# Six transformer layers on one core: a first gathering of expert inputs in fp32, and low parts of weights moved at two joints of four layers

## Chip, core and metric

The kernel runs on one core of a Trainium2 chip. The metric is device time in microseconds (us) of one execution. TensorE multiplies matrices (PE in the profile, its weight loads PEld), VectorE is DVE, ScalarE is ACT, GpSimd is POOL, and SyncE (SP) asks for most transfers.

## What is computed

256 tokens of width 1024 pass through four layers and then two routed ones, all in fp32. Cut to what matters:

```
def first_block(...):
    for i in range(4):
        h = rmsnorm(x, g[0])
        y = diff_attention / nsa_attention / forgetting_attention (h, ...)   # by layer
        x = x + rmsnorm(y, g[1])
        y = sqrelu_mlp(rmsnorm(x, g[2]), mlp_w1[i], mlp_w2[i])        # width 4096
        x = x + rmsnorm(y, g[3])
        x = x + sigmoid(x @ ple_gate_w[i]) * (p[i] @ ple_w[i])

def second_block(...):
    for layer in range(2):
        hcur = rms_norm(x, norm1_g[layer]) * (1 + sc1) + sh1
        x = x + g1 * mixer(hcur)
        hcur = rms_norm(x, norm2_g[layer]) * (1 + sc2) + sh2
        x = x + g2 * hierarchical_moe(hcur, ...)
    return rms_norm(x, final_norm_g)

def hierarchical_moe(...):        # 16 experts; top group of 4, then top 2 in it
    for e in range(16):
        hid = silu(xt @ w_gate[e]) * (xt @ w_up[e])
        y = y + gates[:, e:e + 1] * (hid @ w_down[e])
```

## The kernel before

**Products in parts.** A matrix in fp32 is split into a high part (a rounded copy in the type fp32r, made by ScalarE) and a low part (what is missing, made by VectorE). A product is three products in fp32r: high by high, low by high, high by low. For weights, `whi` is the high part (L270, L277; 128x2048 in one instruction) and `wlo` the low one (L289; two instructions of 128x1024 for one piece, four for a unit of 1024 rows and 512 columns). For activations, `xTh` and `xTl` are evacuated from the PSUM buffer of the transposes (L434): ScalarE copies the high part, VectorE subtracts (both L423).

**Order.** The program is written as Python functions; a scheduler of the framework sets the order of each engine's queue from its own timeline, and `with self.behind(x)` asks it to place what follows after x. Each engine then runs its queue strictly in order.

**The first four layers** (`first_layer`). At the end of the mixer the two halves of 128 tokens are normalised (`enter`: L2202 scales, L2203 adds, into `tm`), transposed and fed to the MLP, whose first products are `mm_a` (L342). `update` (L2208, L2209) adds the mixer's result to the stream x behind that. This is the first joint. The MLP's second matrix is the products `pB<-whi,t` and `pB<-wlo,t` of L308; their sum is normalised in `post_norm` (sum of squares `ss` L396, the reciprocal root L360 to L384, L457 scales, L458 adds to x). x is transposed (L434), and the gate's products (L308 with `whi` or `wlo` and `xTh` or `xTl`) follow. Its first unit of weights is `ug`. This is the second joint.

**The routed layers** (`second_layer`, `moe_pass`). Each half's router logits (L2027) give, on VectorE, the chain of L1593 to L1615 (`route`), then the counts on TensorE (L1627), then 0/1 matrices `Dm` (L1642) that say which token sits in which place. A gathering (`gather`, `collect`, L1675) multiplies columns of X, as stationary operand, with `Dm`: the result, with a shift added by ScalarE (L1682), is `xg`, the transposed inputs of four experts in 256 columns. X is the normalised input in two parts (L2038 high, ScalarE; L2039 low, VectorE), both reordered while being written, so that column block k of X holds the features 8p + k. So a gathering has 8 k x 2 halves x 2 parts = 32 products.

There are 16 experts, two at a time (j = 0 to 7), and a gathering for every two j, four in a layer: the first ahead of j = 0, the second inside j = 1 between the products of gate and up (L1829) and the turn (L1746) to the product down, the third behind j = 3, the fourth inside j = 5. The experts' weights are used in plain fp32 (L1829), with four tiles of 32 columns of the array side by side. They come in pieces of 1 MB (four for gate, up and down each), asked for by SyncE as their buffers come free. A second part of the gathering for experts with more tokens than places (the block under `If` in `rest`) doesn't run in the profiled execution beyond its branch.

Of the kernel before, what the change touches and what calls it, by code (L numbers as in the profile page):

```python
# [21 lines left out]
D = 1024  # L22
# [30 lines left out]
class Net:  # L53
# [396 lines left out]
    def post_norm(self, y, g, h, r2):  # L450
# [4 lines left out]
        r = self.rstd(y, scale=r4, factor=r2)  # L455
        for n, yn in zip(HALVES, y):
            v.scalar_tensor_tensor(yn, yn, r, g[:, n], op0=OP.mult, op1=OP.mult)  # L457
            last = v.tensor_add(self.x[h][:, n], self.x[h][:, n], yn)  # L458
# [1209 lines left out]

    def collect(self, p, X, Dm, b, halves):

        for i in range(2):
            ks = slice((2 * b + i) * 128, (2 * b + i + 1) * 128)
# [114 lines left out]
    def expert_weights(self, l, name, j):  # L1787


        e = [self.expert(j, s) for s in range(2)]  # L1790
        src = self.a[f"moe_w_{name}_2"][l, e[0]:e[1] + 1:e[1] - e[0]]
        pieces = []
        for i in range(4):
            if name != "down":
                tag, n, k0 = "raw" if name == "gate" else "whi", slice(0, 512), 2 * i
                s = src.rearrange("s (p i k) n -> i p s k n", i=4, k=2)[i]
            elif j < 7:
                tag, n, k0 = "wlo", slice(0, D), i
                s = src[:, 128 * i:128 * i + 128].rearrange("s (k p) n -> p s k n", k=1)
            else:  # L1800
                tag, n, k0 = "wlo", HALVES[i // 2], 2 * (i % 2)
                s = src[:, 128 * k0:128 * k0 + 256, n].rearrange("s (k p) n -> p s k n", k=2)
            if name == "gate" and j % 2 and i < 2:
                t = self.xp.tile([128, 2, 2, 512], F32, name="xTl", tag="xTl", bufs=2)
            else:
                t = self.wt(tag, [128, 2, 1 if tag == "wlo" and j < 7 else 2, n.stop - n.start], F32)
            if name == "down" and j == 7:
                for e in range(2):
                    self.nc.sync.dma_start(t[:, e], s[:, e])
            else:  # L1810
                self.nc.sync.dma_start(t, s)
            pieces.append((t, k0, n))
        return pieces
# [19 lines left out]
    def moe_pass(self, l, X, R, sh, g2, first, weights, rest, late, ahead):  # L1833
# [14 lines left out]
        for j in range(8):  # L1848
# [17 lines left out]
            if c and j != 3 and q < 3:  # L1866
# [7 lines left out]
            if j == 6:  # L1874
                late()
            DT, (gs,) = place[j]
# [3 lines left out]
            if j == 3:  # L1880

                self.combine(acc, range(2), j, *out.pop(j))
                rest(acc)
# [6 lines left out]
    def moe_rest(self, l, X, R, sh, g2, base, acc):  # L1890
# [15 lines left out]
        for j in range(8):  # L1906
# [6 lines left out]
            for b in range(4):  # L1913
                p = self.pB([128, 2, 128])
                for i in range(2):
                    ks = slice((2 * b + i) * 128, (2 * b + i + 1) * 128)
                    for k in range(4):
                        h, part = divmod(k, 2)
                        nc.tensor.matmul(p[:, i], X[h][part][:, ks], Dm[:, h], start=k == 0, stop=k == 3)
# [19 lines left out]
    def moe(self, l, X, R, sh, g2, first, weights):  # L1939
# [3 lines left out]
        row = self.one([128, D], "next")  # L1943

        def late():
            self.bcast(self.a["final_norm_g_2"] if l else self.mod[1, D:2 * D], D, row)
# [12 lines left out]
        def rest(acc):  # L1959
# [27 lines left out]
        return update, row  # L1987

    def second_layer(self, l, mix, oT, after):
# [4 lines left out]
        y, begin, end = self.mixed(mix, oT, w, (l, 1 - l))  # L1994
        weights = {"gate": self.expert_weights(l, "gate", 0)}
# [386 lines left out]
```

## Time and profile before

| what | value |
|---|---|
| median of three runs | 2271.1 us (2264.89 to 2271.54) |
| the profiled execution | 2268.48 us, of it 2266.7 us span |
| TensorE (PE) busy | 2104.9 us, 93% |
| VectorE busy | 1346.7 us, 59% |
| ScalarE busy | 937.4 us, 41% |
| moved | 541.67 MB, mean 239 GB/s |

The profile is one execution. "Busy" counts what an engine computed; bracketed times in its rows are idle time just before an instruction, with what ended it. PEclk is the clock granted to TensorE as a share of full speed: 1.00 and 0.50 are its two levels, 2.4 and 1.2 GHz.

### The profile page before, as it was taken

How to read it: one execution, taken by the hardware profiler on the slowest of the kernel's cores; microseconds unless marked ns; L12 is line 12 of the kernel's file. 1: busy time of each engine (PE TensorE's matmuls, PEld its weight loads, DVE VectorE, ACT ScalarE, POOL GpSimd, SP SyncE). 2: the span in 40 equal slices, each digit the busy share in tenths (PEclk: the TensorE clock that was granted, in tenths of full speed). 3: DMA queues.
4: the chain of work that ended last, by engine and by line, in shares of the span. 5: the costliest groups of instructions: out<-in, count | busy, mean ns of one | idle time of the engine just before them, and what ended most of it. 6: DMA issues, size and time to landing. Idle time of an engine off the chain costs nothing. (4 is left out here: it accounts for less than half of the span.)

```text
span 2266.7 us, 35540 instructions
## 1 busy us (share of the span) xinstructions
PE 2104.9 (93%) x14072; PEld 1608.8 (71%) x14072; DVE 1346.7 (59%) x2794; ACT 937.4 (41%) x1464; POOL 25.2 (1%) x69
## 2 busy tenths in 40 slices
PE   7989999989999999999999899989898988989897
PEld 5868888976788878788888698978743327864332
DVE  4578767575877665877666787677611027851112
ACT  4545435455543455544445444446411115521111
POOL 0000000000000010000000000000000001000000
PEclk9999999999999999999999999999999998999999
DMA  8527774630587464477564387656599984469995
GB/s 296 182 74 253 268 257 171 212 121 29 191 279 278 169 217 155 173 260 267 202 229 161 87 284 261 215 205 205 225 407 418 420 353 155 152 246 420 418 419 225
DMA packets 246362, 541.67 MB, mean 239 GB/s; under 512 B 27501, under 2 KB 77189, under 8 KB 246181
## 3 DMA queue, kind: packets, MB, share of 16 engines
q1 hardware_dynamic: 242597, 533.98, 65.3%
q10 hardware_dynamic: 3552, 5.24, 0.6%
q8 instruction: 116, 1.90, 0.3%
q14 instruction: 65, 0.53, 0.1%
q0 software_dynamic: 32, 0.02, 0.0%
HBM read 533.36 MB, written 5.83 MB: 238 GB/s over the span
## 5 line engine op out<-in xcount | busy, mean ns | idle before, releaser
L289 DVE TENSOR_TENSOR wlo<-raw,whi 128x1024 fp32r<-128x1024 f32 x476 | 558.5, 1221 | 223.9 <-ACT whi L270 201.8
L270 ACT CAST whi<-raw 128x2048 fp32r<-128x2048 f32 x218 | 411.1, 1907 | 417.9 <-PE pB L308 336.8
L308 PE MATMUL pB<-whi,t 128*128 128x512 f32 x1088 | 308.1, 401 | 4.7 <-ACT t L423 3.2
L308 PE MATMUL pB<-xTl,whi 128*128 128x256 f32 x1600 | 257.0, 285 | 0.0
L308 PE MATMUL pB<-xTh,whi 128*128 128x256 f32 x1600 | 254.9, 288 | 0.4 <-ACT whi L270 0.4
L308 PE MATMUL pB<-xTh,wlo 128*128 128x256 f32 x1600 | 250.2, 284 | 0.0
L308 PEld LDWEIGHTS pB<-whi,t 128*128 128x128 f32 x1088 | 202.0, 191 | 49.0 <-ACT t L423 4.1
L308 PEld LDWEIGHTS pB<-xTh,whi 128*128 128x128 f32 x1600 | 218.8, 193 | 11.8 <-issue 8.6
L308 PEld LDWEIGHTS pB<-xTl,whi 128*128 128x128 f32 x1600 | 223.2, 193 | 5.3 <-issue 2.3
L308 PEld LDWEIGHTS pB<-xTh,wlo 128*128 128x128 f32 x1600 | 217.8, 192 | 2.7 <-issue 1.7
L308 PE MATMUL pB<-wlo,t 128*128 128x512 f32 x544 | 170.9, 395 | 0.0
L308 PE MATMUL pB<-whi,xTh 128*128 128x512 f32 (+1 forms) x512 | 145.0, 409 | 11.4 <-ACT xTh L423 9.3
L308 PE MATMUL pB<-whi,xTl 128*128 128x512 f32 (+1 forms) x512 | 143.5, 402 | 10.1 <-DVE xTl L423 6.7
L308 PE MATMUL pB<-wlo,xTh 128*128 128x512 f32 (+1 forms) x512 | 139.9, 395 | 0.0
L1195 DVE SCALAR_TENSOR_TENSOR adac<-adaw,cs,adac 128x512 f32<-128x512 f32 x168 | 125.8, 749 | 21.5 <-DMA adaw<-in_w_ada_dram 19.0
L1829 PE MATMUL pB<-wlo,t 128*32 128x512 f32 (+1 forms) x1024 | 116.6, 594 | 11.7 <-ACT t L1747 11.7
L1753 DVE SCALAR_TENSOR_TENSOR t<-pB,gs,g 128x512 f32<-128x512 f32 x32 | 24.0, 751 | 166.2 <-PE pB L1829 164.6
L308 PEld LDWEIGHTS pB<-whi,xTh 128*128 128x128 f32 x512 | 95.4, 197 | 37.2 <-ACT xTh L423 15.2
L308 PEld LDWEIGHTS pB<-whi,xTl 128*128 128x128 f32 x512 | 96.9, 198 | 34.6 <-DVE xTl L423 8.7
L308 PEld LDWEIGHTS pB<-wlo,t 128*128 128x128 f32 x544 | 103.0, 189 | 24.1
L1829 PE MATMUL pB<-whi,xg 128*32 128x512 f32 (+1 forms) x1024 | 114.4, 593 | 0.0
L308 PEld LDWEIGHTS pB<-wlo,xTh 128*128 128x128 f32 x512 | 96.0, 194 | 21.6 <-issue 2.7
(384 smaller groups left out, 2375.9 us busy)
## 6 DMA issues: line engine op xcount, KB each, us to landing
raw<-in_mlp_w_dram SPq DMA_DIRECT2D x128, 1024.0 KB
whi<-in_moe_w_up_dram SPq DMA_DIRECT2D x64, 1024.0 KB
wlo<-in_moe_w_down_dram SPq DMA_DIRECT2D x56, 1024.0 KB
adaw<-in_w_ada_dram SPq DMA_DIRECT2D x96, 512.0 KB
raw<-in_moe_w_gate_dram SPq DMA_DIRECT2D x48, 1024.0 KB
raw<-in_da_w_in_dram SPq DMA_DIRECT2D x24, 1024.0 KB
raw<-in_ple_gate_w_dram SPq DMA_DIRECT2D x16, 1024.0 KB
xTl<-in_moe_w_gate_dram SPq DMA_DIRECT2D x16, 1024.0 KB
```

What stands on the lines that cost most here:

```text
L270: done = nc.scalar.copy(hi, raw)
L289: last = subtract(lo[:, ks], raw[:, ks], hi[:, ks].bitcast(F32), OP.subtract)
L308: self.last_mm = self.nc.tensor.matmul(ps, l, r, start=start and i == 0, stop=stop and i == n - 1)
L1195: v.scalar_tensor_tensor(acc, t[:, i], self.cs[:, k + i:k + i + 1], acc, op0=OP.mult, op1=OP.add)
L1753: self.nc.vector.scalar_tensor_tensor(t, p, gs, g2[:, n], op0=OP.mult, op1=OP.mult)
L1829: self.last_mm = self.nc.tensor.matmul(out[u][es], xT[:, k0 + k, es], t[:, s, k, c], start=done[u] == 1, stop=done[u] == total[u], tile_po ...
```

## The change

Three things are changed.

**At the first joint**, the four L289 of the MLP's first unit `u1` leave the chain of `enter`: they stood ahead of a sum of squares and between the two adds L2203; now they are asked for behind the last transposes of the second half. Scaling and adding alternate (L2232, L2233 in the new numbering).

**At the second joint**, the four L289 of the gate's first unit `ug` are asked for behind the last add of `post_norm` to the first half; they stood ahead of `post_norm`. Here too scaling and adding alternate.

**In the routed layers**, X stays one fp32 matrix for each half, in the stream's own order of features, made by ScalarE alone (contiguous). The first gathering multiplies it in fp32: 16 products in the place of 32. The two parts are made later, at j = 1 (`in_parts`), and serve the other gatherings. Since X is no longer reordered, each gathering reads its stationary operand at a step of 8 elements (`some_rows`), the later ones too. The gathering of j = 1 goes behind the product down. Two of the gate's pieces for j = 1 are asked for early, one into the buffer that `in_parts` uses later; the row that was broadcast into a tile of its own ("next") goes into a recycled buffer of X.

```
-    def unit_apart(self, w, c0):
+    def unit_apart(self, w, c0, first=(), then=()):
         raws = [self.load(w[k * 512:(k + 1) * 512, c0:c0 + 512]) for k in range(2)]
-        u = [self.high(raw, 4 * k) for k, raw in enumerate(raws)]
-        for p, raw in zip(u, raws):
-            self.low(p, raw)
+        with self.behind(*first):
+            u = [self.high(raw, 4 * k) for k, raw in enumerate(raws)]
+        with self.behind(*then):
+            for p, raw in zip(u, raws):
+                self.low(p, raw)
...
+    def some_rows(x, k):
+        return x.rearrange("t (p k) -> t k p", k=8)[:, k]
+
+    def in_parts(self, X):
+        hi = self.one([128, 2, D], "hi", F32R)
+        parts = []
+        for h in range(2):
+            self.nc.scalar.copy(hi[:, h], X[h])
+            lo = self.one([128, D], "X", F32R, bufs=3)
+            self.nc.vector.tensor_tensor(lo, X[h], hi[:, h].bitcast(F32), OP.subtract)
+            parts.append([hi[:, h], lo])
+        return parts
...
-                for part in range(2):
-                    self.nc.tensor.matmul(p[:, i], X[h][part][:, ks], Dm[:, h].rearrange("p c s -> p (c s)"),
-                                          start=h == i == part == 0, stop=h == part == 1, skip_group_check=True)
+                places = Dm[:, h].rearrange("p c s -> p (c s)")
+                if len(X[h]) == 1:
+                    places = places.bitcast(F32)
+                for n, x in enumerate(X[h], 1):
+                    self.nc.tensor.matmul(p[:, i], self.some_rows(x, 2 * b + i), places, start=h == i == 0 and n == 1,
+                                          stop=h == 1 and n == len(X[h]), skip_group_check=True)
...
-            if c and j != 3 and q < 3:
+            if j == 1:
+                X = self.in_parts(X)
+            elif c and j != 3 and q < 3:
                 Dm, xg = self.whole(self.gather(R, X, sh, q + 1))
...
+            if j == 1:
+                Dm, xg = self.whole(self.gather(R, X, sh, q + 1))
+                put(q + 1)
...
         weights = {"gate": self.expert_weights(l, "gate", 0)}
+        self.asked["gate", 1, 0] = self.expert_piece(l, "gate", 1, 0)
...
+            self.asked["gate", 1, 2] = self.expert_piece(l, "gate", 1, 2)
...
-            X = [[self.one([128, D], f"X{h}{part}", F32R) for part in range(2)] for h in range(2)]
+            X = [self.one([128, D], "X", bufs=3) for h in range(2)]
...
-                x = xG[h].rearrange("t (p k) -> t k p", k=8)
-                hi, lo = (t.rearrange("t (k p) -> t k p", k=8) for t in X[h])
-                nc.scalar.mul(hi, x, r[h])
-                v.scalar_tensor_tensor(lo, x, r[h], hi.bitcast(F32), op0=OP.mult, op1=OP.subtract)
...
+            with self.behind(copied):
+                nc.scalar.mul(X[0], xG[0], r[0])
...
-            with self.behind(self.weighted):
-                for u, raw in zip(u1, raws):
-                    self.low(u, raw)
...
             last = self.transpose_in(xg[1], mT, 1)
             with self.behind(*last):
+                for u, raw in zip(u1, raws):
+                    self.low(u, raw)
                 update(y, 0, r0)
...
-            self.post_norm(Y[0], g3, 0, r2[0])
-            with self.behind(*last):
-                ug = [self.unit_apart(self.a["ple_gate_w"][i], 0)]
+            normed = self.post_norm(Y[0], g3, 0, r2[0])
+            ug = [self.unit_apart(self.a["ple_gate_w"][i], 0, last, normed)]
```

VectorE at the second joint of layer 0, before; `x_80` is x of the first half. The four L289 of `ug` stand as one row ahead of all of these:

```order
L457 SCALAR_TENSOR_TENSOR pB<-pB,ry_3380,tm 128x512 x2
L458 TENSOR_TENSOR x_80<-x_80,pB 128x512
L396 TENSOR_TENSOR ss<-ss 128x1
L458 TENSOR_TENSOR x_80<-x_80,pB 128x512
L360 TENSOR_SCALAR rx_3448<-ss,r_3439 128x1
L362 TENSOR_SCALAR rt_3449<-rx_3448 128x1
L364 TENSOR_SCALAR ry_3450<-rt_3449 128x1
L369 SCALAR_TENSOR_TENSOR rh_3451<-ry_3450,rx_3448 128x1
L423 TENSOR_TENSOR xTl<-pB,xTh 128x4x128
```

The same place after the change:

```order
L461 SCALAR_TENSOR_TENSOR pB<-pB,ry_3380,tm 128x512
L462 TENSOR_TENSOR x_80<-x_80,pB 128x512
L461 SCALAR_TENSOR_TENSOR pB<-pB,ry_3380,tm 128x512
L462 TENSOR_TENSOR x_80<-x_80,pB 128x512
L289 TENSOR_TENSOR wlo<-raw,whi 128x1024 x4
L398 TENSOR_TENSOR ss<-ss 128x1
L425 TENSOR_TENSOR xTl<-pB,xTh 128x4x128 x2
L289 TENSOR_TENSOR wlo<-raw,whi 128x1024 x2
```

The four L289 now stand between the second add to x and the two `xTl`, ahead of the second half's sum of squares `ss`.

VectorE at the first joint of layer 0, before (`t_1484` and `t_1487` are the scaled halves of the first 128 tokens' row):

```order
L2202 SCALAR_TENSOR_TENSOR t_1484<-pB,ry_1472,tm 128x512
L2202 SCALAR_TENSOR_TENSOR t_1487<-pB,ry_1472,tm 128x512
L2203 TENSOR_TENSOR tm<-tm,t_1484 128x512
L289 TENSOR_TENSOR wlo<-raw,whi 128x1024 x2
L2203 TENSOR_TENSOR tm<-tm,t_1487 128x512
```

After, first the same place and, behind the line of dots, what follows the last `xTl` of this joint:

```order
L2232 SCALAR_TENSOR_TENSOR t_1484<-pB,ry_1472,tm 128x512
L2233 TENSOR_TENSOR tm<-tm,t_1484 128x512
L2232 SCALAR_TENSOR_TENSOR t_1487<-pB,ry_1472,tm 128x512
L2233 TENSOR_TENSOR tm<-tm,t_1487 128x512
...
L425 TENSOR_TENSOR xTl<-pB,xTh 128x4x128 x2
L289 TENSOR_TENSOR wlo<-raw,whi 128x1024 x4
L2238 SCALAR_TENSOR_TENSOR pB<-pB,ry_1472,tm 128x512 x2
```

The low parts have left the first half's chain and stand behind both halves' operands, ahead of `update`.

TensorE at the first gathering of layer 4, before, where `X_15245` and `X_15246` are the first half's two parts and alternate in the eight products that stand here:

```order
L1627 MATMUL pB<-rmask,rc_15218 128x8
L1627 MATMUL pB<-rmask,rc_15222 128x8
L1675 MATMUL pB<-Dm,X_15245 128x256
L1675 MATMUL pB<-Dm,X_15246 128x256
```

After:

```order
L1631 MATMUL pB<-rmask,rc_15220 128x8
L1631 MATMUL pB<-rmask,rc_15224 128x8
L1697 MATMUL pB<-Dm,X 128x256 x4
L1631 MATMUL pB<-rmask,rc_15218 128x8
L1631 MATMUL pB<-rmask,rc_15222 128x8
```

One product in fp32 stands where two in fp32r stood.

## Rows read from the trace of the kernel before

**Rows 1.** The page, part 1: busy time of each engine over the whole span.

```profile
PE 2104.9 (93%) x14072; PEld 1608.8 (71%) x14072; DVE 1346.7 (59%) x2794; ACT 937.4 (41%) x1464; POOL 25.2 (1%) x69
```

**Rows 2.** Timeline, VectorE and TensorE, layer 0, MLP end to gate: start, us, what, [idle <-releaser].

```profile
359.64 4.69 DVE L289 TENSOR_TENSOR wlo<-raw,whi 128x1024 fp32r<-128x1024 f32 x4 [3.79 <-ACT whi L277]
...
368.82 0.68 DVE L458 TENSOR_TENSOR x<-x,pB 128x512 f32<-128x512 f32 x1
...
370.17 0.68 DVE L423 TENSOR_TENSOR xTl<-pB,xTh 128x512 fp32r<-128x512 f32 x1
...
371.03 1.08 PE L308 MATMUL pB<-whi,xTl 128*128 128x512 f32 x4
...
381.91 1.98 PE L308 MATMUL pB<-whi,xTh 128*128 128x512 f32 x8
```

**Rows 3.** Timeline, the same place of layer 1.

```profile
772.74 4.63 DVE L289 TENSOR_TENSOR wlo<-raw,whi 128x1024 fp32r<-128x1024 f32 x4 [5.42 <-ACT whi L277]
...
780.95 1.28 DVE L458 TENSOR_TENSOR x<-x,pB 128x512 f32<-128x512 f32 x2
...
794.97 1.98 PE L308 MATMUL pB<-whi,xTh 128*128 128x512 f32 x8
```

**Rows 4.** Timeline, the same place of layer 3.

```profile
1487.29 1.28 DVE L458 TENSOR_TENSOR x<-x,pB 128x512 f32<-128x512 f32 x2
...
1501.33 2.01 PE L308 MATMUL pB<-whi,xTh 128*128 128x512 f32 x8
```

**Rows 5.** Timeline, mixer's end to MLP, in layers 0, 1 and 3.

```profile
157.57 1.19 PE L308 MATMUL pB<-whi,xTl 128*128 128x512 f32 x4 [1.74 <-DVE rx L360]
...
161.13 2.35 DVE L289 TENSOR_TENSOR wlo<-raw,whi 128x1024 fp32r<-128x1024 f32 x2
...
164.23 0.63 PE L434 MATMUL pB<-ident,tm 128*128 128x128 f32 x4 [2.29 <-DVE ss L396]
...
584.43 0.63 PE L434 MATMUL pB<-ident,tm 128*128 128x128 f32 x4 [2.24 <-DVE ss L396]
...
1284.07 1.21 PE L308 MATMUL pB<-whi,xTl 128*128 128x512 f32 x4 [1.74 <-DVE rx L360]
...
1290.72 0.63 PE L434 MATMUL pB<-ident,tm 128*128 128x128 f32 x4 [2.26 <-DVE ss L396]
```

**Rows 6.** Busy time by stretch, start of layer 0's MLP: us, PE, PEld, DVE, ACT, POOL, PEclk, DMA share, GB/s.

```profile
174.00:200.00 26.00, 25.71 (x178) 23.71 (x177) 22.46 (x47) 14.57 (x16) 0.62 (x2) 1.00 0.65 218
```

**Rows 7.** Timeline, both routed layers from router to first experts.

```profile
1628.52 2.05 DVE L2039 SCALAR_TENSOR_TENSOR X<-tm,ry,X 128x1024 fp32r<-128x1024 f32 x1 [0.49 <-ACT X L2038]
...
1631.72 2.05 PE L1675 MATMUL pB<-Dm,X 128*128 128x256 f32 x8 [3.41 <-DVE rei L1607]
...
1640.27 6.21 PE L1829 MATMUL pB<-raw,xg 128*32 x56 [1.22 <-ACT xg L1682]
...
2010.95 2.07 DVE L2039 SCALAR_TENSOR_TENSOR X<-tm,ry,X 128x1024 fp32r<-128x1024 f32 x1 [0.94 <-ACT X L2038]
...
2017.39 0.59 PE L1627 MATMUL pB<-rmask,rc 128*128 128x8 f32 x2 [4.88 <-DVE rmask L1613]
...
2019.32 2.07 PE L1675 MATMUL pB<-Dm,X 128*128 128x256 f32 x8 [1.34 <-DVE Dm L1642]
...
2027.24 7.07 PE L1829 MATMUL pB<-raw,xg 128*32 x64 [1.44 <-ACT xg L1682]
```

**Rows 8.** Busy time by stretch within the second of them, columns as in rows 6.

```profile
2015.00:2018.00 3.00, 0.59 (x2) 0.50 (x2) 2.96 (x24) 0.34 (x2) 0.00 (x0) 0.50 0.70 287
```

**Rows 9.** Timeline, TensorE, a later gathering and the gates placed behind it.

```profile
1679.47 4.00 PE L1675 MATMUL pB<-Dm,X 128*128 128x256 f32 x32
...
1683.73 0.95 PE L1776 MATMUL pB<-rgate,Dm 128*128 128x1 f32 x8
```

**Rows 10.** Groups by line and shape, ScalarE: count, busy us, mean ns, idle before.

```profile
L394 ACT ACTIVATE junk<-x 128x1024 bf16<-128x1024 f32 x16 | 16.9, 1053 | 11.1 <-DVE x L1160 8.2 <-DMA x<-in_x_dram 2.9
...
L2038 ACT ACTIVATE X<-tm,ry 128x1024 fp32r<-128x1024 f32 x4 | 8.7, 2174 | 2.2 <-DVE ry L384 2.2
```

More of the change, by code (lines that the diff above doesn't have):

```diff
@@ L455, in post_norm @@
         r = self.rstd(y, scale=r4, factor=r2)
+        last = ()
         for n, yn in zip(HALVES, y):
-            v.scalar_tensor_tensor(yn, yn, r, g[:, n], op0=OP.mult, op1=OP.mult)
-            last = v.tensor_add(self.x[h][:, n], self.x[h][:, n], yn)
+            with self.behind(*last):
+                v.scalar_tensor_tensor(yn, yn, r, g[:, n], op0=OP.mult, op1=OP.mult)
+            last = (v.tensor_add(self.x[h][:, n], self.x[h][:, n], yn),)
         return last
@@ L1787, in expert_weights, with expert_piece @@
     def expert_weights(self, l, name, j):
+        return [self.asked.pop((name, j, i), None) or self.expert_piece(l, name, j, i) for i in range(4)]
+    def expert_piece(self, l, name, j, i):
         e = [self.expert(j, s) for s in range(2)]
         src = self.a[f"moe_w_{name}_2"][l, e[0]:e[1] + 1:e[1] - e[0]]
[L1792 to L1812, printed above, removed]
@@ L1813, in expert_weights @@
-        return pieces
+        if name != "down":
+            tag, n, k0 = "raw" if name == "gate" else "whi", slice(0, 512), 2 * i
+            s = src.rearrange("s (p i k) n -> i p s k n", i=4, k=2)[i]
+        elif j < 7:
+            tag, n, k0 = "wlo", slice(0, D), i
+            s = src[:, 128 * i:128 * i + 128].rearrange("s (k p) n -> p s k n", k=1)
+        else:
+            tag, n, k0 = "wlo", HALVES[i // 2], 2 * (i % 2)
+            s = src[:, 128 * k0:128 * k0 + 256, n].rearrange("s (k p) n -> p s k n", k=2)
@@ new lines, in expert_piece @@
+        if name == "gate" and j % 2 and i < 2:
+            t = self.xp.tile([128, 2, 2, 512], F32, name="xTl", tag="xTl", bufs=2)
+        elif name == "gate" and j == 1 and i == 2:
+            t = self.one([128, 2, 2, 512], "hi")
+        else:
+            t = self.wt(tag, [128, 2, 1 if tag == "wlo" and j < 7 else 2, n.stop - n.start], F32)
+        if name == "down" and j == 7:
+            for e in range(2):
+                self.nc.sync.dma_start(t[:, e], s[:, e])
+        else:
+            self.nc.sync.dma_start(t, s)
@@ L1815, in experts @@
+        return t, k0, n
     def experts(self, xT, pieces, whose, out):
@@ L1882, in moe_pass @@
                 self.combine(acc, range(2), j, *out.pop(j))
-                rest(acc)
+                rest(acc, X)
                 Dm, xg = self.whole(self.gather(R, X, sh, q + 1))
@@ L1942, in moe @@
         nc, v = self.nc, self.nc.vector
-        row = self.one([128, D], "next")
+        rows = []
         def late():
-            self.bcast(self.a["final_norm_g_2"] if l else self.mod[1, D:2 * D], D, row)
+            rows.append(self.bcast(self.a["final_norm_g_2"] if l else self.mod[1, D:2 * D], D,
+                                   self.one([128, D], "X", bufs=3)))
         w = self.a["od_w_in_2"][0]
@@ L1957, in ahead, with rest @@
                 self.low_parts.append((self.early[k], raw))
-        def rest(acc):
+        def rest(acc, X):
             n = nc.values_load(R.most, min_val=0, max_val=8)
@@ L1985, in update @@
             self.squares(h, u)
-        return update, row
+        return update, rows[0]
     def second_layer(self, l, mix, oT, after):
@@ L2023, in logits @@
                     nc.tensor.transpose(p[:, j], xG[h][:, k * 128:(k + 1) * 128], self.ident)
-                nc.scalar.copy(xT[:, 4 * u:4 * u + 4, h * 128:(h + 1) * 128], p)
+                last = nc.scalar.copy(xT[:, 4 * u:4 * u + 4, h * 128:(h + 1) * 128], p)
                 for j in range(4):
@@ L2027, in logits @@
                     nc.tensor.matmul(lgs[:, h], xT[:, k, h * 128:(h + 1) * 128], wr[:, k], start=k == 0, stop=k == 7)
+                return last
             r = {}
@@ L2054, in second_layer @@
             self.tick(2)
-            parts(0)
             update(y1[1], 1, 1)
@@ L2067, in second_layer @@
             self.tick(3)
-            parts(1)
+            nc.scalar.mul(X[1], xG[1], r[1])
             self.settle(chain)
@@ L2199, in enter @@
                 r = self.rstd(y)
+                last = ()
                 for n, yn in zip(HALVES, y):
                     t = self.t2([128, 512])
-                    v.scalar_tensor_tensor(t, yn, r, gg[:, n], op0=OP.mult, op1=OP.mult)
-                    v.tensor_add(xg[h][:, n], xg[h][:, n], t)
+                    with self.behind(*last):
+                        v.scalar_tensor_tensor(t, yn, r, gg[:, n], op0=OP.mult, op1=OP.mult)
+                    last = (v.tensor_add(xg[h][:, n], xg[h][:, n], t),)
                 return r
```

12 lines of the change are left out of this document (6 added, 6 removed).

## Prediction

> **What bounds the kernel now.** I read the busy times first: TensorE computes for 2104.9 us of 2266.7, VectorE for 1346.7 [rows 1]. So TensorE is the bound, and a change pays or costs by what it does to the 162 us in which TensorE stands idle, and by work it adds to TensorE itself. Then I read the timelines at the places the change touches, looking at the brackets on TensorE's rows (what it waited for) and at what VectorE did just then. Times below are those of the profiled execution, 2268.5 us; it is 2.6 us under the median of the three runs, 2271.1, and lies inside them. A difference of 0.3%, 6.8 us, is about what a measurement of this kernel can tell from no change.
>
> **The second joint (MLP to gate), four layers.** In layer 0 the four low parts of the gate's first unit run at 359.64 for 4.69 us, after 3.79 us in which VectorE had nothing to do [rows 2]: they filled a hole. Layer 1 shows the same, 4.63 us behind 5.42 us of idleness [rows 3]. After the change they stand between the last add to the first half of x and the two `xTl`, and TensorE, which takes its products in order, wants `xTl` almost at once.
> Layer 0: the last add ends at 368.82 + 0.68 = 369.50 now. With the hole left empty the normalising chain starts 0.5 us sooner and the alternation saves another 0.35, so 368.65. Add 4.69 for the four, 0.15 for the sum of squares and 0.68 for `xTl`: 374.2. The product that reads it began at 371.03; the new order puts four more high-by-high products ahead of it (4 x 0.227 = 0.9 us), so TensorE stands about 2.25 us. It then has 40 products left, 9.1 us, up to 383.3; meanwhile VectorE owes four more low parts (4.7 us), the second half's chain (2 us) and its scaling and adding, which I add up to 385.2 for the whole of x's second half. The second half's products, at 381.91 now, start at about 385.9: **+4.0 us**.
> Layers 1 and 2 repeat one pattern. In layer 1 x is ready at 780.95 + 1.28 = 782.2 now and at 781.65 then; 4.63 for the low parts, 0.9 for sum and `xTl`: 787.2. With 9.1 us of products TensorE comes to 796.35, x's second half at 798.95, the second half's products at 799.5 instead of 794.97 [rows 3]: **+4.5 us each**. In layer 3 [rows 4] x comes at 1488.0 (now 1488.57), `xTl` at 1493.5, the second half's products at 1503.8 instead of 1501.33: **+2.5 us**.
> Sum +15.5. Bounds: only the first stall stays, 4 x 2.3 = +9; or all of the 4.7 us appears four times, +19. A gain is excluded by the order: between x and `xTl` nothing but 4.7 us of VectorE's work was added, and TensorE has about 2 us to do there.
>
> **The first joint (mixer to MLP), four layers.** Here low parts leave a chain that TensorE waits for: 1.74 and 2.29 us in layer 0, 2.24 in layer 1, 1.74 and 2.26 in layer 3 [rows 5]; layer 2 has no such wait. Two low parts take 2.35 us, so these waits go nearly whole, and layer 1 saves 0.26 more: 10.5 us of gain as the bound on one side. The four, 4 x 1.17 = 4.7 us, now stand ahead of `update` and of all low parts of the MLP's next pieces. VectorE is busy 22.5 of the 26 us that follow and TensorE 25.7 [rows 6], and what is left to VectorE lies in gaps of a tenth of a microsecond, so it can't catch up before TensorE needs the next low parts: I find the next piece's some 2.8 us late in layers 0, 1 and 3, and layer 2 loses without having gained. What is late next is thus the second unit's `wlo`. Other end: everything comes back, 4 x 4.7 - 10.5 = +8. I take **0**, the sum of my four replays (-0.9, +0.3, +1.7, -1.0), which lies in the middle.
>
> **The front of the routed layers.** The split by L2039 leaves the chain from router to places. In the second routed layer both its instructions stood in it: 0.94 + 2.07 us, and 2.05 more, ahead of a wait of 4.88 us on TensorE for `rmask` [rows 7]. I put the counts at 2012.5 instead of 2017.39 and the gathering at 2014.4 instead of 2019.32. The price: a product in fp32. The gate's 64 records take 7.07 us, four side by side, so one of 512 columns takes 0.44 us, and there are two for each product: 0.44 us for a product of 256 columns at 2.4 GHz, 0.88 at 1.2. Sixteen are 7.0 us or 14.1. TensorE has been idle there and is granted 0.50 [rows 8]; I let four run at that level and twelve at full clock, 8.8 us, so the gathering ends at 2023.2 and the first gate's product comes at 2024.5 instead of 2027.24: -2.7. In the first routed layer one L2039 with its wait, 2.5 us, stood in the chain before the gathering at 1631.72 [rows 7]; the gathering could start at 1629.3, runs longer, and ends about when it did: -0.3. Together **-3**; all at full clock -7.5, all at half +6.3.
>
> **The later gatherings.** These are six (three in each layer) of 32 fp32r products, and all of them now load their 128 stationary columns at a step of 8 elements, 32 bytes. Today 32 take 4.00 us [rows 9], 0.12 each. The row below has 8 products of one column each, so nearly nothing but loads: (0.95 - 0.24) / 7 = 0.10 us a load. So a load takes as long as the 256 columns behind it, and whatever it gains in length shows. No row has TensorE reading at a step. ScalarE has: L2038 reads at this same step of 8 and takes 2174 ns for 1024 elements, where L394 takes 1053 contiguous [rows 10]; on VectorE L2039 takes 2.07 us [rows 7] for the same 1024, both 2.0 to 2.1 ns an element. Bounds: nothing, if loads hide the step; 128 x 2.07 = 0.265 us a load, 0.145 more for each of 192 products, +28 us. I take the doubling that ScalarE shows, 0.10 to 0.21, so 0.09 over today's 0.12: 192 x 0.09 = **+17 us**. It lies on the bound, between products of experts that follow each other without a pause. (For the first gathering two such loads, 0.42 us, just fit beside 0.44.)
> A rule speaks against this. The Trainium skill (TensorE: Matmul & The Clock Gate, section "LDWEIGHTS (loading the stationary operand)") prices a load by its columns alone, about 107 ns for 128, whatever the operand's layout; rows 9 agree with that figure for contiguous columns, and by it the step would cost nothing. Against it stands the skill's SBUF page (SBUF — State Buffer, section "Door 1: The DMA port swizzle"): SBUF is read in lines of 16 bytes and each step to a new line pays, which ScalarE's and VectorE's rows bear out. By the first rule the sum below is 17 us less.
>
> **The rest.** The gathering of j = 1 behind the product down has the combining of experts' outputs around it, so its evacuation is covered: +0.5 (0 to 3). `in_parts` adds two copies of 1.05 us and two subtractions of 1.2 to engines that idle for most of a pair of experts. The earlier gate pieces and the row in the recycled buffer move 1 MB and 0.5 MB in SyncE's queue; TensorE has been the bound in these layers, so I cost them at nothing.
>
> **Sum.** 15.5 + 0 - 3 + 17 + 0.5 = +30: 2268.5 + 30 = **2298.5 us**.
>
> **Rivals.**
> 1. Loads at a step hide: the sum without that term is +13, **2281.5**. For it: no row shows a load of TensorE slowed by how its operand lies, and TensorE's reading need not be like ScalarE's; against it: two engines pay about double for this step [rows 7, 10]. The Trainium skill's price by columns, named above, is this rival.
> 2. The moved low parts are covered, faster than before. This is one mechanism: VectorE has time for the four where they stand now. Then the first joint keeps 10.5, the second gains what the emptied hole gives (0.85 + 2 x 0.55 + 0.55 = 2.5) and the fronts 3, with loads hidden: -16, **2252.5**. It decides at whether TensorE has at least 5.5 us of other work between x and its first `xTl` product; the order gives it about 2, which speaks against it.
> 3. Half of it: VectorE's delay at the second joint is only partly seen (+9), the first joint keeps half of its gain (-5), fronts -3, loads hidden: +1.5, **2270**, no change that a measurement can tell. That the early pieces do nothing is in the forecast already.
>
> **How the numbers follow.** Forecast 0.48, rival 1 0.28, rival 2 0.12, rival 3 0.12. Forecast and its own bounds give 2286 to 2314; rival 1, with the joints' bounds, 2268 to 2294. The range of 2270 to 2312 leaves out rival 2, half of rival 3 and the upper end of the loads, about 2 in 10. Slower by over 0.3%: the forecast, and 0.24 of rival 1, together 0.72; the same: 0.04 of rival 1 and 0.10 of rival 3, 0.14; faster: 0.14.
>
> **What would show it.** At the second joint, the `xTl` product of the gate's first piece waiting some 2 us for VectorE, and the second half's first product about 4 us later relative to the MLP's end. At the first joint, no waits on `ss` or `rx`, and a new one on `wlo` some 15 us into the MLP. In the second routed layer, counts about 5 us sooner, a gathering of 16 products of 0.44 to 0.88 us. In the later gatherings 32 products in 6.5 to 7 us instead of 4.0. The prediction is wrong if these stay at 4.0 (then rival 1), and badly so if the `xTl` products at the second joint don't wait.

## The result: 1.4% slower, as forecast, by other sizes of the same terms

| kernel | median | lowest to highest | runs |
|---|---|---|---|
| before | 2271.3 us | 2264.9 to 2274.0 | 4 |
| after | 2303.3 us | 2298.1 to 2304.9 | 4 |

The ratio is 1.0141, 95% interval 1.0122 to 1.0161: 32 us slower (28 to 37). The forecast was 2298.5, its range 2270 to 2312. The profiled execution of the changed kernel took 2303.67 us, its span 2301.9, which is 35.2 us longer than the span before; the mean granted clock is 0.973 in both. In the new numbering lines up to L289 are unchanged, L308 is L310, L342 L344, L423 L425, L434 L436, L458 L462, L1627 L1631, L1675 L1697, L1829 L1853.

**Where the time goes.** To see it I laid the starts of the same TensorE instructions of the two traces side by side; the last column is what was gained or lost since the row above.

| TensorE's instruction | before | after | shift | step |
|---|---|---|---|---|
| layer 0, last transposes ahead of the MLP | 173.25 | 166.41 | -6.8 | -6.8 |
| layer 0, last products of the MLP | 367.26 | 362.81 | -4.5 | +2.4 |
| layer 1, first transposes | 392.79 | 394.09 | +1.3 | +5.8 |
| layer 1, last transposes ahead of the MLP | 593.43 | 586.05 | -7.4 | -8.7 |
| layer 1, last products of the MLP | 779.43 | 776.66 | -2.8 | +4.6 |
| layer 2, first transposes | 805.86 | 808.98 | +3.1 | +5.9 |
| layer 2, last transposes ahead of the MLP | 939.56 | 941.46 | +1.9 | -1.2 |
| layer 2, last products of the MLP | 1128.05 | 1133.27 | +5.2 | +3.3 |
| layer 3, first transposes | 1156.12 | 1165.15 | +9.0 | +3.8 |
| layer 3, last transposes ahead of the MLP | 1299.75 | 1302.32 | +2.6 | -6.5 |
| layer 3, last products of the MLP | 1485.77 | 1496.96 | +11.2 | +8.6 |
| first routed layer, first counts L1627 | 1627.73 | 1642.68 | +15.0 | +3.8 |
| first routed layer, first gate product | 1640.27 | 1655.36 | +15.1 | +0.1 |
| second routed layer, first transposes L1231 | 1877.57 | 1903.56 | +26.0 | +10.9 |
| second routed layer, first counts | 2017.39 | 2038.65 | +21.3 | -4.7 |
| second routed layer, first gate product | 2027.24 | 2051.32 | +24.1 | +2.8 |
| last combining | 2254.94 | 2290.12 | +35.2 | +11.1 |

So the two joints together cost 15, the fronts of the routed layers gain 1.8, and the stretches with the later gatherings cost 22. A single step of the table can be off by some 3 us, since stretches of the same work differ between executions: in the kernel before, the granted clock is 0.50 from 324 to 330 us though TensorE was busy throughout and just before, and three kernels of the experiments whose first four layers are those of the kernel before (contiguous columns, steps of 2 and 4) lose 2.6 to 3.0 us against it between 470 and 511 us.

**The later gatherings.** TensorE's timeline in the changed kernel at j = 1 of the first routed layer (start, us, what, idle before in brackets):

```profile
1695.91 7.07 PE L1853 MATMUL pB<-wlo,t 128*32 x64 [0.75 <-ACT t L1769]
1702.92 0.52 PE L1697 MATMUL pB<-Dm,hi 128*128 128x256 f32 x1
1703.27 0.41 PE L1697 MATMUL pB<-Dm,X 128*128 128x256 f32 x1
1703.51 0.41 PE L1697 MATMUL pB<-Dm,hi 128*128 128x256 f32 x1
1703.76 0.41 PE L1697 MATMUL pB<-Dm,X 128*128 128x256 f32 x1
```

The starts lie 0.245 us apart; in [rows 9] 32 such products took 4.00 us, 0.12 each. This gathering of 32 takes 7.8 us. The products behind the first have no bracket: TensorE isn't waiting, it is slower, and so the page shows its busy time up by 30 us rather than its idleness (28 of them in the gatherings, the first ones in fp32 among them):

```profile
PE 2135.0 (93%) x14072; PEld 1631.1 (71%) x14072; DVE 1344.7 (58%) x2794; ACT 939.4 (41%) x1468; POOL 25.5 (1%) x69
```

**The second joint.** Layer 0 of the changed kernel, VectorE and TensorE, which answers to [rows 2]:

```profile
363.44 0.69 DVE L462 TENSOR_TENSOR x<-x,pB 128x512 f32<-128x512 f32 x1
364.04 4.66 DVE L289 TENSOR_TENSOR wlo<-raw,whi 128x1024 fp32r<-128x1024 f32 x4
368.69 1.28 DVE L425 TENSOR_TENSOR xTl<-pB,xTh 128x512 fp32r<-128x512 f32 x2
...
367.37 1.20 PE L310 MATMUL pB<-whi,xTh 128*128 128x512 f32 x4 [1.41 <-ACT whi L270]
369.43 1.70 PE L310 MATMUL pB<-whi,xTl 128*128 128x512 f32 x4 [0.86 <-DVE xTl L425]
```

The order is the forecast one: last add to x, four low parts, `xTl`. TensorE's stall has two names. Of the 2.27 us the first 1.41 are put down to a high part, `whi` L270 on ScalarE; the rest is `xTl`. The four other high-by-high products that the new order puts ahead need the second unit's high part, which ScalarE casts only behind the two `xTh`. That wait was not in my working, but it hides in the one that was: without it TensorE would have waited 1.41 us longer for `xTl`. Behind the wait TensorE runs at half its clock for a while, and the second half's first product (at 381.91 in [rows 2]) comes late; the second row below is the stretch from 370 to 373 (us, busy PE, PEld, DVE, ACT, POOL, PEclk, DMA share, GB/s):

```profile
383.07 2.11 PE L310 MATMUL pB<-whi,xTh 128*128 128x512 f32 x8 [1.38 <-ACT xTh L425]
```

```profile
370.00:373.00 3.00, 3.00 (x8) 2.32 (x7) 2.52 (x4) 1.43 (x1) 0.00 (x0) 0.50 1.05 403
```

**The first joint.** TensorE in layer 0, from the mixer's end into the MLP; [rows 5] answer to the first two of them:

```profile
157.97 1.27 PE L436 MATMUL pB<-ident,tm 128*128 128x128 f32 x8
160.41 2.44 PE L310 MATMUL pB<-whi,t 128*128 128x512 f32 x8 [0.74 <-ACT t L425]
166.41 1.04 PE L436 MATMUL pB<-ident,tm 128*128 128x128 f32 x8
...
184.90 0.73 PE L310 MATMUL pB<-xTh,wlo 128*128 128x256 f32 x4 [1.39 <-DVE wlo L289]
186.04 0.50 PE L310 MATMUL pB<-xTh,wlo 128*128 128x256 f32 x2 [0.40 <-DVE wlo L289]
```

The waits on `rx` and `ss` are gone, and 18 us into the MLP there is the new one on `wlo`, 1.8 us in two rows. In layer 3 the loss is larger and its first cause is no low part but a transfer. TensorE, and ScalarE just before:

```profile
1320.71 3.78 PE L310 MATMUL pB<-whi,t 128*128 128x512 f32 x8 [5.29 <-ACT t L1111]
```

```profile
1317.60 1.90 ACT L270 CAST whi<-raw 128x2048 fp32r<-128x2048 f32 x1 [8.86 <-DMA raw<-in_mlp_w_dram]
```

ScalarE waits 8.86 us for a piece of the MLP's weights, and the activation `t` that TensorE needs stands behind that cast in ScalarE's queue. A low part reads the raw piece; as long as it isn't made, the piece's buffer can't be given to the next transfer (SyncE waits for such low parts 217 times in the changed kernel, 942.9 us in all). SyncE's requests for these pieces, before and after (the two of the second row are the last two of the first), and VectorE's low parts after:

```profile
1294.35 1.69 SPq L239 DMA_DIRECT2D raw<-in_mlp_w_dram x3
```

```profile
1309.35 0.90 SPq L239 DMA_DIRECT2D raw<-in_mlp_w_dram x2
```

```profile
1304.83 4.62 DVE L289 TENSOR_TENSOR wlo<-raw,whi 128x1024 fp32r<-128x1024 f32 x4
```

Before, the piece is asked for 4.9 us ahead of the last transposes of this joint (1299.75), after, 7.0 us behind them (1302.32). Two things stand ahead of the request now: the low parts, of which the first two end at 1307.2, and a run of small requests that keeps SyncE busy up to 1309.26. Which of them holds it, the trace doesn't decide.

**The fronts.** TensorE in the second routed layer, which answers to [rows 7]:

```profile
2038.65 0.39 PE L1631 MATMUL pB<-rmask,rc 128*128 128x8 f32 x2 [0.75 <-DVE rmask L1617]
2040.23 3.78 PE L1697 MATMUL pB<-Dm,X 128*128 128x256 f32 x8 [1.20 <-DVE rei L1611]
2044.52 2.71 PE L1697 MATMUL pB<-Dm,X 128*128 128x256 f32 x8
2047.20 4.18 PE L1697 MATMUL pB<-Dm,X 128*128 128x256 f32 x16
2051.32 4.93 PE L1853 MATMUL pB<-raw,xg 128*32 x44
```

The wait for `rmask` fell from 4.88 to 0.75 us, and 2.8 of the 4.7 us so gained are spent in the gathering in fp32 (there are two records for each product).

### The profile page after: what moved, and what is told of

Same layout as the page of the kernel before. It is cut to its first block, busy times and chain, and to the rows that moved or that the text cites. A ratio compares the mean times of both kernels' runs of the same rounds, so it can differ in the third digit from the quotient of the medians.

```text
span 2301.9 us, 35545 instructions
## 1 busy us (share of the span) xinstructions
PE 2135.0 (93%) x14072; PEld 1631.1 (71%) x14072; DVE 1344.7 (58%) x2794; ACT 939.4 (41%) x1468; POOL 25.5 (1%) x69
## 5 line engine op out<-in xcount | busy, mean ns | idle before, releaser
L289 DVE TENSOR_TENSOR wlo<-raw,whi 128x1024 fp32r<-128x1024 f32 x476 | 558.2, 1222 | 206.9 <-ACT whi L270 206.9
L270 ACT CAST whi<-raw 128x2048 fp32r<-128x2048 f32 x218 | 412.7, 1910 | 453.8 <-PE pB L310 333.4
L310 PE MATMUL pB<-whi,t 128*128 128x512 f32 x1088 | 306.8, 398 | 12.9 <-ACT t L1111 7.5
L310 PE MATMUL pB<-xTl,whi 128*128 128x256 f32 x1600 | 258.9, 286 | 0.0
L310 PE MATMUL pB<-xTh,wlo 128*128 128x256 f32 x1600 | 251.3, 285 | 5.6 <-DVE wlo L289 5.6
L310 PE MATMUL pB<-xTh,whi 128*128 128x256 f32 x1600 | 253.9, 287 | 0.4 <-ACT whi L270 0.4
L310 PEld LDWEIGHTS pB<-whi,t 128*128 128x128 f32 x1088 | 199.7, 190 | 58.7 <-ACT t L1111 8.1
L310 PEld LDWEIGHTS pB<-xTl,whi 128*128 128x128 f32 x1600 | 225.1, 194 | 5.5 <-issue 2.2
L310 PEld LDWEIGHTS pB<-xTh,whi 128*128 128x128 f32 x1600 | 218.7, 193 | 12.2 <-issue 8.9
L310 PEld LDWEIGHTS pB<-xTh,wlo 128*128 128x128 f32 x1600 | 218.5, 193 | 9.2 <-DVE wlo L289 6.9
L310 PE MATMUL pB<-wlo,t 128*128 128x512 f32 x544 | 170.6, 394 | 0.0
L310 PE MATMUL pB<-whi,xTh 128*128 128x512 f32 (+1 forms) x512 | 147.2, 413 | 18.7 <-ACT xTh L425 10.7
L310 PE MATMUL pB<-whi,xTl 128*128 128x512 f32 (+1 forms) x512 | 141.5, 399 | 6.8 <-DVE xTl L425 6.7
L310 PE MATMUL pB<-wlo,xTh 128*128 128x512 f32 (+1 forms) x512 | 140.0, 397 | 0.0
L310 PEld LDWEIGHTS pB<-whi,xTh 128*128 128x128 f32 x512 | 95.8, 199 | 46.3 <-ACT xTh L425 16.2
L1853 PE MATMUL pB<-wlo,t 128*32 128x512 f32 (+1 forms) x1024 | 117.7, 594 | 11.7 <-ACT t L1769 11.7
L310 PEld LDWEIGHTS pB<-wlo,t 128*128 128x128 f32 x544 | 102.4, 188 | 23.9
L310 PEld LDWEIGHTS pB<-whi,xTl 128*128 128x128 f32 x512 | 95.7, 194 | 31.5 <-DVE xTl L425 10.3
L1853 PE MATMUL pB<-whi,xg 128*32 128x512 f32 (+1 forms) x1024 | 115.2, 594 | 0.0
L310 PEld LDWEIGHTS pB<-wlo,xTh 128*128 128x128 f32 x512 | 96.9, 194 | 22.3 <-issue 2.7
```

Source lines behind the costliest of these rows:

```text
L270: done = nc.scalar.copy(hi, raw)
L289: last = subtract(lo[:, ks], raw[:, ks], hi[:, ks].bitcast(F32), OP.subtract)
L310: self.last_mm = self.nc.tensor.matmul(ps, l, r, start=start and i == 0, stop=stop and i == n - 1)
L1853: self.last_mm = self.nc.tensor.matmul(out[u][es], xT[:, k0 + k, es], t[:, s, k, c], start=done[u] == 1, stop=done[u] == total[u], tile_po ...
```

## Experiments

Each kernel ran beside the kernel before, on the same chip; the intervals are those of its own comparison.

**One part at a time.** My theory was that the parts are separate and add up, with the sizes read off above. The rival is that they depend on each other: a shift of VectorE against TensorE at one joint is paid or paid back at another.

*The routed layers alone* (`enter`, `update`, `post_norm` and the two units of weights as before):

```
-            ug = [self.unit_apart(self.a["ple_gate_w"][i], 0, last, normed)]
+            with self.behind(*last):
+                ug = [self.unit_apart(self.a["ple_gate_w"][i], 0)]
...
+            with self.behind(self.weighted):
+                for u, raw in zip(u1, raws):
+                    self.low(u, raw)
```

> Only the part in the routed layers, both joints as before. If the costs are separate: the fronts -2 and six later gatherings at 0.245 us a product instead of 0.12, +22 to +24, so about 20 us slower than before. If the slow gatherings hung on the time shift that the joints make, it would be within 5 us of before.

Measured: 2285.1 us, ratio 1.0078 (1.0061 to 1.0095), +17.7 us.

*The first joint alone*, put into the kernel before:

```
-            with self.behind(self.weighted):
-                for u, raw in zip(u1, raws):
-                    self.low(u, raw)
...
             with self.behind(*last):
+                for u, raw in zip(u1, raws):
+                    self.low(u, raw)
                 update(y, 0, r0)
```

> Only the first joint. The trace of the changed kernel shows about -15 at the joint and +19 inside the MLPs of four layers: if both belong to this edit, between -3 and +4 us against before. Rival: the losses inside the MLPs belong to the second joint's edits, then 10 to 15 us faster.

Measured: 2266.6 us, ratio 0.9998 (0.9989 to 1.0008), no difference. The trace shows both sides: TensorE's waits of this kernel have lost those on `ss` and `rx` and show in their place (engine and line, what it waited for, us in total, times, longest):

```profile
PE pB L308 <- DVE wlo L289: 5.3, 6, 1.5
...
PE pB L308 <- ACT t L1107: 4.1, 1, 4.1
```

*The second joint alone*:

```
-            self.post_norm(Y[0], g3, 0, r2[0])
-            with self.behind(*last):
-                ug = [self.unit_apart(self.a["ple_gate_w"][i], 0)]
+            normed = self.post_norm(Y[0], g3, 0, r2[0])
+            ug = [self.unit_apart(self.a["ple_gate_w"][i], 0, last, normed)]
```

> Only the second joint. By the order and the trace: 3 to 6 us lost in each of four layers, 15 to 18 us slower than before. Rival: with the first joint undone VectorE is ahead of where it was and covers part of it, 5 to 8 us slower.

Measured: 2284.1 us, ratio 1.0075 (1.0058 to 1.0092), +17.0 us. So the three parts are +17.7, -0.5 and +17.0, together 34.2 against 32 (28 to 37) for the whole: they add up, as far as intervals of 2 to 4 us for each part can tell. The rival falls in the second joint's case too: the 5 to 8 us that it gave lie below the interval of 13.1 to 20.9.

**Why the gatherings are slow.** Theory: the step of 8 in the stationary operand. Rival: their new place behind the product down, or the shared buffers. The edit, on the kernel with the routed part alone, stores X reordered and reads contiguous columns; all else stays moved:

```
-        return x.rearrange("t (p k) -> t k p", k=8)[:, k]
+        return x[:, k * 128:(k + 1) * 128]
...
-                nc.scalar.mul(X[0], xG[0], r[0])
+                nc.scalar.mul(X[0].rearrange("t (k p) -> t k p", p=128), xG[0].rearrange("t (p k) -> t k p", k=8), r[0])
```

> Only the part in the routed layers, with one thing undone: X is stored reordered, so that every gathering reads contiguous columns (ScalarE reads at a step of 8 while it makes X, about 1 us more each time). If the step makes the gatherings slow, they take 4.0 us again and the time is within 4 us of before. If it is their new place or their operands' buffers, it stays about 20 us slower.

Measured: 2266.1 us, ratio 0.9992 (0.9982 to 1.0002). The whole 17.7 us are gone, and the rival with them. Then the step itself, with X stored so that the columns of one block lie 2 or 4 elements apart (the pattern `t (a p b) -> t a b p` with b = 2 or 4 in the two places):

> Only the part in the routed layers, with X stored so that the gatherings read at a step of 2 elements (8 bytes) instead of 8. If a load pays for each new line of 16 bytes, a product takes somewhere between 0.12 and 0.245 us, near 0.12 if two elements of a line are enough. If any step at all costs the full price, 0.245 us.

> The same with a step of 4 elements (16 bytes). By lines of 16 bytes every column is on a new line, as at a step of 8: 0.245 us a product, the time as with the step of 8 (18 us slower than before). If the price grows with the step, about half of the extra: 0.18 us a product.

Measured, one execution each: 2268.8 us with a step of 2, and 2290.3 with a step of 4. The groups of TensorE's weight loads for the later gatherings (count, busy us, mean ns of one), contiguous, step 2, step 4 and step 8, in this order, one kernel each:

```profile
L1693 PEld LDWEIGHTS pB<-Dm,hi 128*128 128x128 f32 x96 | 21.1, 220 | 17.4 <-issue 15.6 <-PE pB L1849 1.7
```

```profile
L1693 PEld LDWEIGHTS pB<-Dm,hi 128*128 128x128 f32 x96 | 21.4, 223 | 17.5 <-issue 15.7 <-PE pB L1849 1.7
```

```profile
L1693 PEld LDWEIGHTS pB<-Dm,hi 128*128 128x128 f32 x96 | 31.6, 329 | 17.4 <-issue 15.7 <-PE pB L1849 1.7
```

```profile
L1693 PEld LDWEIGHTS pB<-Dm,hi 128*128 128x128 f32 x96 | 32.2, 336 | 17.4 <-issue 15.6 <-PE pB L1849 1.7
```

The price is not proportional to the step: 220, 223, 329 and 336 ns. Between 8 and 16 bytes lies the jump, and beyond it hardly anything is added. The starts of the products show the same: 0.12, 0.12, 0.23 and 0.24 us apart at full clock.

**Why the first joint gives nothing.** Theory: the low parts stand one step too late; where VectorE was idle for 4.40 us ahead of the last two `xTl` they would cost nothing and free their raw pieces in time. The hole in layer 0 of the kernel before, VectorE:

```profile
174.56 1.29 DVE L423 TENSOR_TENSOR xTl<-pB,xTh 128x512 fp32r<-128x512 f32 x2 [4.40 <-ACT xTh L423]
```

Rival: VectorE is late in the MLP wherever they stand. The edit, in the kernel before, with alternating scaling and adding in `enter`, which keeps its last add as `added[h]`:

```
-            with self.behind(self.weighted):
-                for u, raw in zip(u1, raws):
-                    self.low(u, raw)
...
             r1 = enter(y1, 1)
+            with self.behind(*added[1]):
+                for u, raw in zip(u1, raws):
+                    self.low(u, raw)
             self.ple_proj(pc, pT)
```

> Only the first joint, with the four low parts asked for one step sooner: behind the last add of the second half, ahead of its last two xTl, where VectorE stood idle for 4.4 us before. If the loss inside the MLPs comes from the low parts standing behind the xTl and holding their raw pieces, the waits on wlo in the MLPs go and the 15 us of gain at the joint stay in part: 5 to 14 us faster than before. Rival: the MLPs lose because VectorE is late whatever the place: within 3 us of before.

Measured: 2253.4 us, ratio 0.9939 (0.9922 to 0.9955), 13.8 us faster. VectorE and TensorE at the joint of layer 0 in this kernel:

```profile
166.32 4.63 DVE L289 TENSOR_TENSOR wlo<-raw,whi 128x1024 fp32r<-128x1024 f32 x4
170.86 1.28 DVE L423 TENSOR_TENSOR xTl<-pB,xTh 128x512 fp32r<-128x512 f32 x2
...
168.51 4.10 PE L342 MATMUL pB<-xTh,whi 128*128 128x256 f32 x32 [0.29 <-ACT xTh L423]
172.45 4.00 PE L342 MATMUL pB<-xTl,whi 128*128 128x256 f32 x32
```

The first `xTl` is ready before 172, and TensorE comes to its products at 172.45, after 32 others: the low parts are covered by 4 us of products that need only `xTh`. TensorE has no wait on `wlo` left in its list. Laid beside the trace of the kernel with the first joint as changed, the four MLPs are 2.2, 2.4, 5.3 and 1.8 us shorter, 11.7 together, where 13 lie between the medians of the two. The transfer in layer 3 is freed in part only. ScalarE's wait for the raw piece, in the kernel with the first joint as changed and, for the same piece and the one behind it, in this one:

```profile
1298.39 1.90 ACT L270 CAST whi<-raw 128x2048 fp32r<-128x2048 f32 x1 [8.95 <-DMA raw<-in_mlp_w_dram]
```

```profile
1286.53 1.91 ACT L270 CAST whi<-raw 128x2048 fp32r<-128x2048 f32 x1 [4.37 <-DMA raw<-in_mlp_w_dram]
...
1290.38 1.90 ACT L270 CAST whi<-raw 128x2048 fp32r<-128x2048 f32 x1 [1.45 <-DMA raw<-in_mlp_w_dram]
```

The low parts still stand later than in the kernel before, the piece is asked for 3.8 us behind the last transposes, and TensorE's wait on `t` there falls only from 4.07 to 3.28 us.

**Is it the place at the second joint?** Against the kernel with the second joint alone, only the place of the four low parts is undone; scaling and adding still alternate:

```
-            normed = self.post_norm(Y[0], g3, 0, r2[0])
-            ug = [self.unit_apart(self.a["ple_gate_w"][i], 0, last, normed)]
+            self.post_norm(Y[0], g3, 0, r2[0])
+            ug = [self.unit_apart(self.a["ple_gate_w"][i], 0, last, last)]
```

> Only the second joint with one thing undone: the four low parts of the gate's first unit are free to run ahead of the first half's normalisation again; scaling and adding still alternate. If their place costs the 17 us, the time is within 3 us of before (up to 3 faster by the alternation). If the alternation or the order of TensorE's products costs it, it stays 10 to 17 us slower.

Measured: 2268.6 us, ratio 1.0006 (0.9996 to 1.0015). The low parts are back in the hole and the loss is gone; the alternation alone is worth nothing that can be measured:

```profile
353.58 4.70 DVE L289 TENSOR_TENSOR wlo<-raw,whi 128x1024 fp32r<-128x1024 f32 x4 [3.79 <-ACT whi L277]
```

**A version that beats both.** The early low parts at the first joint, the second joint as before, and the routed part with contiguous columns:

> The early low parts at the first joint together with the part in the routed layers with contiguous columns; the second joint as before. If the pieces add up, 13.5 us for the joint and about 1 for the rest: 2252, 14 to 15 us faster than before. If the routed part gives nothing, 13 us, as the joint alone.

Measured: 2252.8 us, ratio 0.9936 (0.9921 to 0.9950). And with X kept in the stream's order for the first gathering, reordered only while the two parts are made:

```
+            x, u = X[h].rearrange("t (p k) -> t k p", k=8), hi[:, h].rearrange("t (k p) -> t k p", p=128)
+            self.nc.scalar.copy(u, x)
...
+            self.nc.vector.tensor_tensor(lo.rearrange("t (k p) -> t k p", p=128), x, u.bitcast(F32), OP.subtract)
```

> As the other, but X stays in the stream's order for the first gathering in fp32 (read at a step of 8) and is reordered while the two parts are made at j = 1, so that only the later gatherings read contiguous columns. The fronts should gain 0.3 to 0.5 us in each routed layer against the other kernel, whose ScalarE reads at a step while it makes X; 0 to 1 us in all.

Measured: 2252.1 us, ratio 0.9930 (0.9916 to 0.9943), 16 us faster than the kernel before. In its first routed layer the first gate product starts 12.57 us after the counts, against 13.03 in the kernel just above:

```profile
1611.27 0.47 PE L1627 MATMUL pB<-rmask,rc 128*128 128x8 f32 x2 [0.75 <-DVE rmask L1613]
...
1623.84 7.08 PE L1850 MATMUL pB<-raw,xg 128*32 x64
```

That is the 0.3 to 0.5 us that was expected there. In the second routed layer the expectation fails: the gate product starts 12.34 us after the counts, against 11.51, later and not sooner; why was not looked into. The two kernels' totals can't be told apart, nor from the first joint's edit alone (0.9939). What the routed part is worth with contiguous columns stays open: between nothing and a few us.

## Why the prediction was right, point by point

**Second joint, +15.5 forecast.** Alone it costs 17.0 us (13.1 to 20.9), and putting back the low parts' place takes it all away. The mechanism is the one that was worked out from the order and the rows: 4.7 us of VectorE's work between x and `xTl`, where TensorE has about 2 us to do. The stall of 2.25 us forecast for layer 0 is 1.41 + 0.86 = 2.27 in the trace. From the MLP's last products to the second half's first product the four layers are 5.6, 4.2, 3.7 and 2.8 us longer, 16.3 together, where 4.0, 4.5, 4.5 and 2.5 were forecast. Two things were missed. One is the name of the stall's first part: moving the low parts also let the scheduler put products of the second unit ahead, and those wait for ScalarE. The other is the clock, which makes layer 0 the dearest: the 40 products behind the stall, priced at 9.1 us, took 10.8, the first of them at a granted clock of 0.50.

**First joint, 0 forecast, -0.5 measured alone.** The net was right, both sides of it were too small, and that they cancel all the same is luck. The bound on the gain was 10.5, the sum of the brackets; the trace shows more. From the last products ahead of the waits (153.72 before, 152.39 after) to the last transposes ahead of the MLP, layer 0 gains 5.5 us where its two waits are 4.0. The difference is mostly the clock: after those waits TensorE ran at half of it, and now it doesn't. That is no accident of one execution: the seven kernels here with this joint as before all show the lower level on these products, and the five with the low parts moved do not. The stretch from 166 to 170 us before, and the one from 160 to 164 after, which hold the same eight products (us, busy PE, PEld, DVE, ACT, POOL, PEclk, DMA share, GB/s):

```profile
166.00:170.00 4.00, 3.98 (x10) 3.13 (x11) 3.86 (x11) 0.00 (x0) 0.00 (x0) 0.57 0.90 310
```

```profile
160.00:164.00 4.00, 3.59 (x14) 2.54 (x15) 3.72 (x14) 0.96 (x2) 0.00 (x0) 1.00 0.78 270
```

Those eight took 3.52 us before and take 2.44. On the other side the late `wlo`, forecast at 2.8 us, is 1.8 in layer 0 (1.39 + 0.40), but the four MLPs lose 2.4 to 8.6 us. The largest loss, in layer 3, begins with a raw piece that comes late. That step was missing: the working followed the readers of what moves, not the buffers that it reads nor the requests that wait for them. That the low parts hold the piece's buffer is argued from the order; it isn't shown apart from SyncE's other requests. The other step that was missing is the clock again. In layer 1 the waits on `wlo` and `t` add up to 2.5 of the 4.6 us lost, and most of the rest is a stretch behind the waits on `wlo` at the lower level:

```profile
605.00:609.00 4.00, 3.61 (x19) 3.40 (x18) 4.00 (x6) 1.56 (x3) 0.00 (x0) 0.57 0.98 382
```

**Later gatherings, +17 forecast, 19.3 in the traces.** Right in kind, and near in size by two errors of opposite sign. I doubled the time of a load (0.21), where the rows of ScalarE and VectorE gave 2.0 to 2.1 ns an element (0.265 for 128 columns). Measured is 0.245 us, 1.9 ns a column, nearer to the second. With that price the term would have been 192 x 0.125 = 24 and the forecast 2305.5. But the 0.12 us of the kernel before holds for four of the six gatherings only. The one behind j = 3 does not follow other products without a pause: TensorE has stood idle, runs at the lower clock, and needs 0.21 us a product without any step. Before (the row and its stretch) and after:

```profile
1751.14 6.83 PE L1675 MATMUL pB<-Dm,X 128*128 128x256 f32 x32 [5.73 <-PEq L1961]
```

```profile
1751.00:1756.00 5.00, 4.86 (x23) 4.89 (x23) 0.51 (x3) 1.05 (x3) 0.00 (x0) 0.50 1.02 411
```

```profile
1772.00:1776.00 4.00, 4.00 (x18) 4.00 (x18) 0.00 (x0) 0.58 (x2) 0.00 (x0) 0.50 1.03 411
```

Added up from the starts, these two gatherings cost 1.4 and 2.0 us more after the change and the other four 3.9 to 4.0 each, 19.3 together; the remaining 2.7 of the table's 22 are the place of the gathering, below. Of the two rules set against each other, the Trainium skill's price by columns alone (TensorE: Matmul & The Clock Gate, section "LDWEIGHTS (loading the stationary operand)") holds for contiguous columns and for a step of 2 (0.12 us a product) and fails from a step of 4 on (0.23). The Trainium skill's lines of 16 bytes (SBUF — State Buffer, section "Door 1: The DMA port swizzle"), which want two accesses each for full bandwidth, give just that: at a step of 2 elements there are two in a line, at 4 and 8 one.

**Fronts, -3 forecast, -1.8 in the trace.** In the second routed layer the counts come 4.7 us sooner (forecast 4.9), and 2.8 of it goes into the dearer products (forecast 2.2). The first breaks even, as forecast.

**The rest.** The gathering of j = 1 behind the product down was put at +0.5 (0 to 3) and cost 2.7, 1.3 to 1.4 us in each layer; the kernel with contiguous columns loses the same there, though its fronts give it back (0.9992). Of this, 0.90 us is a wait at j = 2 that the kernel before doesn't have. There the combining of the experts' outputs (L1763, now L1785) stood between the products and the turn, and VectorE had its time for `t` under it; now it stands beside the gathering, and nothing covers `t`. Before and after:

```profile
1706.67 2.14 PE L1763 MATMUL pB<-tm,DT 128*128 128x512 f32 x8
1708.64 0.60 PE L1746 MATMUL pB<-ident,t 128*128 128x128 f32 x4
```

```profile
1728.72 0.63 PE L1768 MATMUL pB<-ident,t 128*128 128x128 f32 x4 [0.90 <-DVE t L1887]
```

One shift in the table is no part of my working: of the step of -8.7 in layer 1 the joint has 4.2, and 4.5 lie in the mixer ahead of it, between 394 and 565 us, which the change doesn't touch. The only thing I found there is that the granted clock of the stretch from 445 to 485 is 0.96 instead of 0.91; some 3 us is what kernels with the same order differ by in this mixer, and I leave it open.

## What to carry to other kernels

An operand's layout belongs to its price: where a weight load is as long as the product behind it, reading the stationary operand at a step of 16 bytes or more doubled the product here, and no wait shows it, only the busy time. A price read from one row holds for the state of that row: the same gathering elsewhere ran at half the clock and had less to lose. Work moved off a chain should land in a hole of its engine that was there before, and a hole is found by looking at the brackets of that engine, not at the chain alone: four low parts a layer cost 17 us when they were moved out of a hole at the second joint, and saved 14 when they were moved into one at the first. When work is moved later, follow what it reads as well as who reads it: the buffers that it holds can delay the next transfer.

## What the runs showed of the hardware that I had not expected

- The jump in the load's price lies between a step of 8 and one of 16 bytes (223 and 329 ns a load, 0.12 and 0.23 us a product), and a step of 32 bytes adds almost nothing (336 ns).
- At a step of 32 bytes a product takes the same 0.245 us at either granted clock (1.00 and 0.50), where contiguous columns give 0.12 and 0.21: at the lower clock the step costs 0.03 us, not 0.12.
- A wait of 2.3 us after one of 1.7 cost 1.1 us more in the eight products behind it, which ran at a granted clock of 0.57 on average. The sum of brackets is not the upper bound of what taking them away can give.
